# Encoder kernel: the evacuations of one plain pair moved behind the next pair's copies, and the last tile finished in three column pieces

## The chip, the cores and the metric

The kernel runs on one core of one Trainium2 chip. The metric is device time in microseconds for one launch; the number given for a kernel is the median of several runs.

## The reference

One encoder layer over two request groups, 1024 sample rows and 256 prompt rows of width 1024, all in float32. What matters here are the last two of its steps:

```python
h2 = rms_norm(x, norm_mlp_g) * (1 + scale2) + shift2
x = x + gate2 * (jnp.square(jax.nn.relu(h2 @ w_mlp_up)) @ w_mlp_down)
return rms_norm(x, final_g)      # x * rsqrt(mean(x*x) + 1e-6) * final_g
```

`w_mlp_up` is 1024 x 4096 and `w_mlp_down` 4096 x 1024. Everything ahead of them (modulation, input projection, convolution branch, attention branch, output projection) is the same in both kernels.

## The kernel before, in words

Every float32 operand of a product is split into a high part (a rounded copy, ScalarE, helper `hi_lo` line 156) and a low part (the difference, VectorE or GpSimd, line 160), and each product is three matmuls: high x high, high x low, low x high. The order of the instructions on every engine is the order in which the program emits them; there is no scheduler. Each engine works its own list in that order, and so do the two lists of transfers that SyncE (`nc.sync.dma_start`) and ScalarE (`nc.scalar.dma_start`) issue.

**The up projection** (lines 1263 to 1545) handles its 32 blocks of 128 hidden columns in pairs. The 1280 rows are three chunks: 0 and 1 of 512 rows, 2 of 256. Pairs 0 and 1 are *plain*: eight k-steps of three matmuls for each of the chunks, one bank of PSUM for each output, with `po[f, c]` for block f and chunk c, and `pm1` for chunk 2 of both blocks of pair 1. Pairs 2 to 15 (`up_pair`, line 1445) use seven products of halves instead of eight (a Strassen form): their operands are the raw pieces A and B of the weight, the sums S12 and S34 of pieces (`p_sum`, split by `p_split`), and the row operands T1, T2, T3, T4 (combinations of pieces of the activations, made by `t_first` and `t_third`). T3 is written over `Mh[1]`, `Ml[1]`, so `t_third(k)` can only run when the plain products have read those.

An evacuation `up_out` is a Relu and a Square on ScalarE from PSUM into a tile `r` (lines 1317, 1318) and one transfer issued from ScalarE's own list (line 1323); `up_out_c2` does the same for chunk 2, with two transfers (line 1329). `t_third(k)` is two sums on VectorE (`b_raw`, line 1381), a difference there (line 1415), the high copy on ScalarE (line 1392) and the low part on VectorE (line 1393, deferred until `t_lo`).

The order around the change is: `p_split(2, False)`, `t_third(0)`, `up_out_c2(1, pm1)`, `p_sum(2, True)`, `t_lo()`, `up_out(2, 0, ...)`, and then pair 2. In a pair, TensorE forms X from the first half of A, and ScalarE copies X to `p1` (line 1455); TensorE does half of the chunk 2 products (24 matmuls of 256 columns) and only then adds more products into the same bank X, for which `p1` must have been read. The products Y (S12 x T2) and V (S12 x T1) follow; VectorE reads Y with `p1` into `u2` (line 1465), and TensorE then adds S34 x T3 into the same bank Y, for which `u2` must have been read. Between the products the function `after(step)` (line 1518) emits the preparation of the same and of the next pair. In pair 2 it also emits the rest of pair 1's work:

```python
            if i == 2 and step == 0:
                up_out(3, 0, po[3, 0])
                t_third(1); t_third(2); t_lo()
            elif i == 2 and step == 1:
                t_third(3); t_lo()
            if step == 0:
                p_split(i, True)          # high half ScalarE, low half VectorE for i < 3
```

(three calls are put on one line here). `after(1)` comes behind the evacuation of X and ahead of Y.

**The down projection** (`mlp_down`, line 1567) sums over groups of hidden blocks into ten accumulators `acc[t]`, one for each tile of 128 rows. In the last group, of five blocks, `finish(t, pds)` (line 1621) also adds the two PSUM banks, multiplies by the gate `gb`, adds the residual `base[t]`, and normalises: a Square with a row sum on ScalarE (line 1608, for the last tile 1633), mean and power -0.5 on GpSimd (lines 180, 181, for the last tile 1635, 1638 and 1639) and one VectorE operation `(acc * rs) * fg` (`fin_out`, line 1617), followed by the store that SyncE issues (line 1619). The normalisation of a tile is emitted one or two tiles later. For the last tile (t = 9) the bank of columns 0 to 511 is filled first (15 matmuls of 512 columns), then that of 512 to 1023, and the VectorE steps run on each half; `fin_out(8)` stands behind them, and `fin_out(9, 2)` works and stores the last tile in two halves.

Of the kernel before, what the change touches and what calls it, by code (L numbers as in the profile page):

```python
# [13 lines left out]
D = 1024  # L14
# [11 lines left out]
EPS = 1e-6  # L26
# [44 lines left out]
def encoder_kernel(tc, x_prompt, x_sample, c_prompt, c_sample, ada_w, ada_b, norm_mix_g, w_in,  # L71
# [1357 lines left out]
        up_out(2 + fi, 1, po[2 + fi, 1])  # L1429
    p_split(2, False)  # L1430
    t_third(0)
    up_out_c2(1, pm1)
    p_sum(2, True)
    t_lo()
    up_out(2, 0, po[2, 0])

    def prod(out, w, at_, xh, xl, first, last, more=False):

# [76 lines left out]
    for i in range(2, NP):  # L1515
        last = i == NP - 1

        def after(step, i=i, last=last):
            if i == 2 and step == 0:
                up_out(3, 0, po[3, 0])  # L1520
                t_third(1)
                t_third(2)
                t_lo()
            elif i == 2 and step == 1:
                t_third(3)
                t_lo()
            if step == 0:
                p_split(i, True)
                if last:
                    wd_load(0)  # L1530
                    wd_load(1)
                    g_load(0)
                else:
                    p_load(i + 1)
            elif step == 1:
                wd_split(0) if last else p_ab(i + 1, 0)
            elif step == 2:
                g_load(1) if last else p_sum(i + 1, False)
            elif step == 3:
                g_split(0) if last else p_sum(i + 1, True)  # L1540
            elif step == 4:
                wd_split(1) if last else p_ab(i + 1, 1)
            elif not last:
                p_split(i + 1, False)
        up_pair(i, after)
# [20 lines left out]
    def mlp_down(fs, evac, between, early=0):  # L1566

        nf = len(fs)
        ws = {}
        steps = [(t, range(3)) for t in range(early)] + [(t, range(3, nf)) for t in range(early)]  # L1570
        steps += [(t, range(nf)) for t in range(early, NT)]
        banks = {}
        for n, (t, part) in enumerate(steps):
            o = t * 128
            if t not in banks:
                banks[t] = [bank("b", "dn_ps", 8) for _ in range(2)]
            pds = banks[t]
            order = [(i, hf) for i in part for hf in range(2)] if early and t == 0 else \
                [(i, hf) for hf in range(2) for i in part]
            for i, hf in order:  # L1580
                if i not in ws:
                    ws[i] = dn.pop(("W", fs[i]))
                gh, gl_ = (g[:, o:o + 128] for g in dn["G", fs[i]])
                wdh, wdl = (w[:, hf * 512:hf * 512 + 512] for w in ws[i])
                for s, (l_, r_) in enumerate(((gh, wdh), (gh, wdl), (gl_, wdh))):
                    nc.tensor.matmul(pds[hf], lhsT=l_, rhs=r_, start=(i == 0 and s == 0), stop=(i == nf - 1 and s == 2),  # L1586
                                     skip_group_check=bool(early))
            if part[-1] == nf - 1:
                evac(t, pds)
            between(n)  # L1590
        for f in fs:
            dn.pop(("G", f))
# [28 lines left out]
    def finish(t, pds):  # L1621
        gb = g2[0 if t < 8 else 1]
        if t >= 1:
            fin_norm(t - 1)
        if t == NT - 1:
            ss = co.tile([128, 4], F32, tag="sums", name="ss2", bufs=3)
            sq = fp.tile([128, D], F32, tag="sq", name="sq", bufs=2)
            for hf in range(2):
                cs = slice(hf * 512, hf * 512 + 512)
                nc.vector.tensor_add(acc[t][:, cs], acc[t][:, cs], pds[hf])  # L1630
                nc.vector.tensor_mul(acc[t][:, cs], acc[t][:, cs], gb[:, cs])
                nc.vector.tensor_add(acc[t][:, cs], acc[t][:, cs], base[t][:, cs])
                nc.scalar.activation(sq[:, cs], acc[t][:, cs], AF.Square, accum_out=ss[:, hf:hf + 1])
                if hf == 0:
                    nc.gpsimd.tensor_scalar(ss[:, 2:3], ss[:, 0:1], 1.0 / D, EPS, op0=ALU.mult, op1=ALU.add)
            fin_out(t - 1)
            rs = co.tile([128, 1], F32, tag="rs", name="rs", bufs=8)
            nc.gpsimd.tensor_scalar(rs, ss[:, 1:2], 1.0 / D, ss[:, 2:3], op0=ALU.mult, op1=ALU.add)
            nc.gpsimd.tensor_tensor(rs, rs, neghalf[:, 0:1], op=ALU.pow)
            fin[t] = rs  # L1640
            fin_out(t, 2)
            return
        for hf in range(2):
            cs = slice(hf * 512, hf * 512 + 512)
            nc.vector.tensor_add(acc[t][:, cs], acc[t][:, cs], pds[hf])
            if t >= 2 and hf == 0:
                fin_out(t - 2)
        nc.vector.tensor_mul(acc[t], acc[t], gb)
        (nc.vector if t == NT - 2 else nc.gpsimd).tensor_tensor(acc[t], acc[t], base[t], op=ALU.add)
        if t == NT - 2:  # L1650
            fin_out(t - 1)
        base_load(t + 3)

    chunks = [[0]] + [[f, f + 1] for f in range(1, NF - 5, 2)] + [list(range(NF - 5, NF))]
# [79 lines left out]
```

## Time and profile before

| what | value |
|---|---|
| median of three runs | 1894.7 us (1893.22 to 1895.27) |
| time of the profiled execution | 1894.61 us |
| its span, first to last instruction | 1892.8 us |
| TensorE matmul busy | 1842.3 us, 97% of the span |
| TensorE weight load busy | 1537.4 us, 81% |
| VectorE, ScalarE, GpSimd busy | 1082.7, 682.0, 625.6 us |
| mean granted TensorE clock | 0.991 |
| moved by DMA | 207.55 MB, 110 GB/s on average |

Engines are PE (TensorE matmul), PEld (its weight load), DVE (VectorE), ACT (ScalarE), POOL (GpSimd) and SP (SyncE); a name with q behind it is the engine's sequencer, which issues transfers. Matmuls are pipelined, so a matmul's own time is longer than the distance from its start to the next one's. In a row of the timeline the first number is the start in us from the span's start, the second the time; in brackets stands how long the engine was idle before, and what ended that. A group's idle time says who came last by the profile.

### The profile page before, as it was taken

How to read it: one execution, taken by the hardware profiler on the slowest of the kernel's cores; microseconds unless marked ns; L12 is line 12 of the kernel's file. 1: busy time of each engine (PE TensorE's matmuls, PEld its weight loads, DVE VectorE, ACT ScalarE, POOL GpSimd, SP SyncE). 2: the span in 40 equal slices, each digit the busy share in tenths (PEclk: the TensorE clock that was granted, in tenths of full speed). 3: DMA queues.
4: the chain of work that ended last, by engine and by line, in shares of the span. 5: the costliest groups of instructions: out<-in, count | busy, mean ns of one | idle time of the engine just before them, and what ended most of it. 6: DMA issues, size and time to landing. Idle time of an engine off the chain costs nothing.

```text
span 1892.8 us, 24497 instructions
## 1 busy us (share of the span) xinstructions
PE 1842.3 (97%) x9468; PEld 1537.4 (81%) x9468; DVE 1082.7 (57%) x1420; ACT 682.0 (36%) x1132; POOL 625.6 (33%) x467
## 2 busy tenths in 40 slices
PE   5999999999999999999999999999999999999998
PEld 2888777888997888877788878888888888888886
DVE  3799996524436777777555753333334555555557
ACT  3411111221346877774233454444444111111112
POOL 3321121421321343334022024333345444234443
PEclk7999999999999999999999999999999999999999
DMA  8313452227131211117632233222226332233224
GB/s 313 112 44 106 173 185 99 70 96 254 51 86 74 54 44 39 47 49 226 208 123 79 84 103 98 98 92 95 95 87 210 115 100 80 71 101 101 75 93 154
DMA packets 120934, 207.55 MB, mean 110 GB/s; under 512 B 10946, under 2 KB 78355, under 8 KB 119794
## 3 DMA queue, kind: packets, MB, share of 16 engines
q1 hardware_dynamic: 103106, 167.32, 27.6%
q10 hardware_dynamic: 17712, 38.67, 5.2%
q8 instruction: 74, 1.21, 0.3%
q14 instruction: 42, 0.34, 0.1%
HBM read 151.83 MB, written 54.12 MB: 109 GB/s over the span
## 4 chain that ended last, share of the span: by engine, by line
PE 54%; DVE 4%; DMA 3%; ACT 2%; issue 1%; POOL 1%; SPq 0%; ACTq 0%; DVEq 0%; POOLq 0%
PE dn_ps L1586 23%; PE up_ps L1442 13%; PE wo_ps L1198 4%; PE tp L866 2%; PE up_ps L330 2%; PE up_ps L329 2%; PE up_ps L328 2%; PE ops L881 1%; PE ops L880 1%; PE S L851 1%; PE S L850 1%; PE S L852 1%; DMA ga<-sig_a 1%; DMA m<-m_d 1%; DMA orr<-o_d 1%
## 5 line engine op out<-in xcount | busy, mean ns | idle before, releaser
L160 POOL TENSOR_TENSOR wl<-wr,wh 128x1024 fp32r<-128x1024 f32 (+1 forms) x100 | 232.0, 2321 | 759.6 <-ACT wh L156 729.5
L1601 DVE TENSOR_TENSOR acc<-acc,dn_ps 128x512 f32<-128x512 f32 x260 | 178.8, 688 | 174.8 <-PE dn_ps L1586 174.8
L1586 PE MATMUL dn_ps<-wh,gl 128*128 128x512 f32 x640 | 249.1, 389 | 0.9 <-POOL gl L160 0.9
L1586 PE MATMUL dn_ps<-wl,gh 128*128 128x512 f32 x640 | 249.0, 389 | 0.0
L1586 PE MATMUL dn_ps<-wh,gh 128*128 128x512 f32 x640 | 249.0, 389 | 0.0
L156 ACT ACTIVATE wh<-wr 128x1024 fp32r<-128x1024 f32 (+1 forms) x104 | 102.9, 991 | 381.8 <-PE dn_ps L1586 290.5
L412 DVE SCALAR_TENSOR_TENSOR z<-u,dwt,z 128x1310 f32<-128x1310 f32 x120 | 220.8, 1840 | 4.3
L328 PE MATMUL fma<-Hh,wh 128*128 128x512 f32 x384 | 154.7, 403 | 0.3 <-DVE Hh L158 0.3
L329 PE MATMUL fma<-Hl,wh 128*128 128x512 f32 x384 | 150.4, 392 | 2.0 <-DVE Hl L160 2.0
L330 PE MATMUL fma<-Hh,wl 128*128 128x512 f32 x384 | 150.4, 392 | 0.0
L1586 PEld LDWEIGHTS dn_ps<-wh,gl 128*128 128x128 f32 x640 | 120.1, 188 | 26.2 <-POOL gl L160 1.4
L1586 PEld LDWEIGHTS dn_ps<-wl,gh 128*128 128x128 f32 x640 | 120.1, 188 | 25.1
L1586 PEld LDWEIGHTS dn_ps<-wh,gh 128*128 128x128 f32 x640 | 120.1, 188 | 24.8
L160 DVE TENSOR_TENSOR Pl<-tp,Ph 128x512 fp32r<-128x512 f32 x144 | 92.8, 650 | 20.2 <-ACT Ph L156 19.0
L160 POOL TENSOR_TENSOR gl<-gr,gh 128x1280 fp32r<-128x1280 f32 x32 | 94.3, 2947 | 12.5 <-DMA up_d<-r 9.7
L328 PE MATMUL up_ps<-Mh,wh 128*128 128x256 f32 (+1 forms) x320 | 97.4, 304 | 0.8 <-ACT hf L266 0.8
L329 PE MATMUL up_ps<-Ml,wh 128*128 128x256 f32 (+1 forms) x320 | 97.4, 304 | 0.0
L330 PE MATMUL up_ps<-Mh,wl 128*128 128x256 f32 (+1 forms) x320 | 97.4, 304 | 0.0
L156 ACT ACTIVATE Ph<-tp 128x512 fp32r<-128x512 f32 x144 | 82.4, 574 | 35.9 <-PE tp L866 33.2
L1442 PE MATMUL up_ps<-Mh,wh 128*128 128x512 f32 x224 | 87.5, 391 | 4.3 <-ACT p L1455 2.4
L328 PEld LDWEIGHTS fma<-Hh,wh 128*128 128x128 f32 x384 | 72.5, 189 | 23.2 <-issue 5.0
L1442 PE MATMUL up_ps<-Ml,wh 128*128 128x512 f32 x224 | 87.3, 390 | 0.0
(327 smaller groups left out, 4285.4 us busy)
## 6 DMA issues: line engine op xcount, KB each, us to landing
gr<-up_d SPq DMA_DIRECT2D x32, 640.0 KB
adr<-in_ada_w_dram SPq DMA_DIRECT2D x32, 512.0 KB
wr<-in_w_mlp_up_dram SPq DMA_DIRECT2D x32, 512.0 KB
up_d<-r ACTq DMA_DIRECT2D x64, 256.0 KB
wr<-in_w_mlp_down_dram SPq DMA_DIRECT2D x32, 512.0 KB
wr<-in_w_in_dram SPq DMA_DIRECT2D x24, 512.0 KB
ar<-in_ada_w_dram SPq DMA_DIRECT2D x8, 1024.0 KB
sig_a<-sgg ACTq DMA_DIRECT2D x8, 640.0 KB
```

Source lines behind the costliest of these rows:

```text
L156: nc.scalar.activation(h, raw, AF.Copy)
L160: e.tensor_tensor(l, raw, h.bitcast(F32), op=ALU.subtract)
L328: nc.tensor.matmul(o, lhsT=wh, rhs=xh, start=first, stop=False)
L329: nc.tensor.matmul(o, lhsT=wh, rhs=xl, start=False, stop=False)
L330: nc.tensor.matmul(o, lhsT=wl, rhs=xh, start=False, stop=last)
L412: nc.vector.scalar_tensor_tensor(out=z[j], in0=u[j][:, t:t + ZW], scalar=dwt[:, j, t:t + 1], in1=z[j], op0=ALU.mult, op1=ALU.add)
L850: nc.tensor.matmul(S[:, b:b + e], lhsT=Qh[:, qs], rhs=Kh[:, kk], start=True, stop=False)
L866: nc.tensor.transpose(tp[:, i * 128:(i + 1) * 128], st_[n]["P"][i][:, k * 128:(k + 1) * 128], ident)
L1198: nc.tensor.matmul(pp[hf], lhsT=a, rhs=wo[k][b][:, hf * 512:hf * 512 + 512], start=(k == 0 and s == 0), stop=(k == KD - 1 and s == 2))
L1442: nc.tensor.matmul(out, lhsT=l_, rhs=r_[:, k, :], start=(a and s == 0), stop=(b and s == 2), skip_group_check=more)
L1586: nc.tensor.matmul(pds[hf], lhsT=l_, rhs=r_, start=(i == 0 and s == 0), stop=(i == nf - 1 and s == 2), skip_group_check=bool(early))
L1601: nc.vector.tensor_add(acc[t][:, cs], acc[t][:, cs], pds[hf])
```

## The change

In pair 2 three evacuations of pair 1 move to later places in the lists: that of chunk 2 (`up_out_c2(1, pm1)`) and of block 2 (`up_out(2, 0)`) from ahead of the pair into `after(0)` and `after(1)`, behind the T3 copies there, and that of block 3 (`up_out(3, 0)`) from the head of `after(0)` to `after(2)`. In the last tile, the second bank's products are issued as two column quarters, each over all five blocks (256 columns a matmul), and the VectorE and ScalarE steps run on a half and two quarters. Tile 8's product with `fg` moves to VectorE at the end of its own `finish`, and ScalarE scales it and SyncE stores it at the head of the last tile's `finish`. The last tile's `(acc * rs) * fg` becomes a product with `fg` on VectorE, and then a scaling of columns 512 to 1023 on ScalarE (stored from its own list) beside one of columns 0 to 511 on VectorE (stored by SyncE).

```diff
--- before.py
+++ after.py
@@ -1429,10 +1429,8 @@
         up_out(2 + fi, 1, po[2 + fi, 1])
     p_split(2, False)
     t_third(0)
-    up_out_c2(1, pm1)
     p_sum(2, True)
     t_lo()
-    up_out(2, 0, po[2, 0])
 
     def prod(out, w, at_, xh, xl, first, last, more=False):
 
@@ -1517,13 +1515,16 @@
 
         def after(step, i=i, last=last):
             if i == 2 and step == 0:
-                up_out(3, 0, po[3, 0])
                 t_third(1)
                 t_third(2)
                 t_lo()
+                up_out_c2(1, pm1)
             elif i == 2 and step == 1:
                 t_third(3)
                 t_lo()
+                up_out(2, 0, po[2, 0])
+            elif i == 2 and step == 2:
+                up_out(3, 0, po[3, 0])
             if step == 0:
                 p_split(i, True)
                 if last:
@@ -1577,6 +1578,8 @@
             pds = banks[t]
             order = [(i, hf) for i in part for hf in range(2)] if early and t == 0 else \
                 [(i, hf) for hf in range(2) for i in part]
+            if early and t == NT - 1:
+                order = [(i, 0) for i in part]
             for i, hf in order:
                 if i not in ws:
                     ws[i] = dn.pop(("W", fs[i]))
@@ -1585,6 +1588,14 @@
                 for s, (l_, r_) in enumerate(((gh, wdh), (gh, wdl), (gl_, wdh))):
                     nc.tensor.matmul(pds[hf], lhsT=l_, rhs=r_, start=(i == 0 and s == 0), stop=(i == nf - 1 and s == 2),
                                      skip_group_check=bool(early))
+            if early and t == NT - 1:
+                for lo in (512, 768):
+                    for i in part:
+                        gh, gl_ = (g[:, o:o + 128] for g in dn["G", fs[i]])
+                        wdh, wdl = (w[:, lo:lo + 256] for w in ws[i])
+                        for s, (l_, r_) in enumerate(((gh, wdh), (gh, wdl), (gl_, wdh))):
+                            nc.tensor.matmul(pds[1][:, lo - 512:lo - 256], lhsT=l_, rhs=r_, start=(i == 0 and s == 0),
+                                             stop=(i == nf - 1 and s == 2), skip_group_check=True)
             if part[-1] == nf - 1:
                 evac(t, pds)
             between(n)
@@ -1625,20 +1636,29 @@
         if t == NT - 1:
             ss = co.tile([128, 4], F32, tag="sums", name="ss2", bufs=3)
             sq = fp.tile([128, D], F32, tag="sq", name="sq", bufs=2)
-            for hf in range(2):
-                cs = slice(hf * 512, hf * 512 + 512)
-                nc.vector.tensor_add(acc[t][:, cs], acc[t][:, cs], pds[hf])
+            eps = co.tile([128, 1], F32, name="eps")
+            nc.scalar.activation(base[t - 1], base[t - 1], AF.Copy, scale=fin[t - 1])
+            nc.sync.dma_start(y_rows(t - 1), base[t - 1])
+            for i, cs in enumerate((slice(0, 512), slice(512, 768), slice(768, 1024))):
+                p0 = cs.start % 512
+                nc.vector.tensor_add(acc[t][:, cs], acc[t][:, cs], pds[cs.start // 512][:, p0:p0 + cs.stop - cs.start])
                 nc.vector.tensor_mul(acc[t][:, cs], acc[t][:, cs], gb[:, cs])
                 nc.vector.tensor_add(acc[t][:, cs], acc[t][:, cs], base[t][:, cs])
-                nc.scalar.activation(sq[:, cs], acc[t][:, cs], AF.Square, accum_out=ss[:, hf:hf + 1])
-                if hf == 0:
-                    nc.gpsimd.tensor_scalar(ss[:, 2:3], ss[:, 0:1], 1.0 / D, EPS, op0=ALU.mult, op1=ALU.add)
-            fin_out(t - 1)
+                nc.scalar.activation(sq[:, cs], acc[t][:, cs], AF.Square, accum_out=ss[:, i:i + 1])
+                if i == 0:
+                    nc.gpsimd.tensor_scalar(eps, ss[:, 0:1], 1.0 / D, EPS, op0=ALU.mult, op1=ALU.add)
+                elif i == 1:
+                    nc.gpsimd.tensor_scalar(eps, ss[:, 1:2], 1.0 / D, eps, op0=ALU.mult, op1=ALU.add)
             rs = co.tile([128, 1], F32, tag="rs", name="rs", bufs=8)
-            nc.gpsimd.tensor_scalar(rs, ss[:, 1:2], 1.0 / D, ss[:, 2:3], op0=ALU.mult, op1=ALU.add)
+            nc.gpsimd.tensor_scalar(rs, ss[:, 2:3], 1.0 / D, eps, op0=ALU.mult, op1=ALU.add)
             nc.gpsimd.tensor_tensor(rs, rs, neghalf[:, 0:1], op=ALU.pow)
             fin[t] = rs
-            fin_out(t, 2)
+            fg_x = base[t]
+            nc.vector.tensor_mul(fg_x, acc[t], fg)
+            nc.scalar.activation(fg_x[:, 512:1024], fg_x[:, 512:1024], AF.Copy, scale=rs)
+            nc.scalar.dma_start(y_rows(t)[:, 512:1024], fg_x[:, 512:1024])
+            nc.vector.tensor_scalar(fg_x[:, 0:512], fg_x[:, 0:512], rs, None, op0=ALU.mult)
+            nc.sync.dma_start(y_rows(t)[:, 0:512], fg_x[:, 0:512])
             return
         for hf in range(2):
             cs = slice(hf * 512, hf * 512 + 512)
@@ -1649,6 +1669,7 @@
         (nc.vector if t == NT - 2 else nc.gpsimd).tensor_tensor(acc[t], acc[t], base[t], op=ALU.add)
         if t == NT - 2:
             fin_out(t - 1)
+            nc.vector.tensor_mul(base[t], acc[t], fg)
         base_load(t + 3)
 
     chunks = [[0]] + [[f, f + 1] for f in range(1, NF - 5, 2)] + [list(range(NF - 5, NF))]
```

## Rows read from the trace of the kernel before

**Rows 1.** The waits of TensorE over the whole span: who waited for whom, total us, times, longest us.

```profile
PE up_ps L1442 <- ACT p L1455: 2.4, 1, 2.4
...
PE up_ps L1442 <- DVE u L1465: 1.9, 1, 1.9
```

**Rows 2.** The timeline of TensorE's matmuls at the start of pair 2.

```profile
1097.73 0.28 PE L328 MATMUL up_ps<-Mh,wh 128*128 128x256 f32 x1
...
1100.48 0.28 PE L330 MATMUL up_ps<-Mh,wl 128*128 128x256 f32 x1
1103.12 0.50 PE L1442 MATMUL up_ps<-Mh,wh 128*128 128x512 f32 x1 [2.36 <-ACT p L1455]
...
1111.19 0.39 PE L1442 MATMUL up_ps<-T1h,wl 128*128 128x512 f32 x1
1113.52 0.47 PE L1442 MATMUL up_ps<-Mh,wh 128*128 128x512 f32 x1 [1.95 <-DVE u L1465]
```

**Rows 3.** The timeline of ScalarE in the same stretch (ACTq is its list of transfers).

```profile
1098.62 0.58 ACT L1317 ACTIVATE r<-up_ps 128x512 f32<-128x512 f32 x1
...
1099.89 0.81 ACTq L1329 DMA_DIRECT2D up_d<-r  x2
1100.80 0.60 ACT L1317 ACTIVATE r<-up_ps 128x512 f32<-128x512 f32 x1 [0.94 <-ACT r L1318]
...
1102.47 0.60 ACT L1455 ACTIVATE p<-up_ps 128x512 f32<-128x512 f32 x1 [0.40 <-ACT r L1318]
...
1106.62 0.63 ACT L1392 ACTIVATE Mh<-br 128x512 fp32r<-128x512 f32 x1 [1.36 <-DVE br L1415]
1107.15 1.04 ACT L156 ACTIVATE wh<-sr 128x1024 fp32r<-128x1024 f32 x1
```

**Rows 4.** The timeline of VectorE in the same stretch.

```profile
1101.09 0.69 DVE L1415 TENSOR_TENSOR br<-br,u 128x512 f32<-128x512 f32 x1
...
1105.29 0.69 DVE L1393 TENSOR_TENSOR Ml<-br,Mh 128x512 fp32r<-128x512 f32 x1 [2.18 <-ACT Mh L1392]
1105.89 0.69 DVE L1415 TENSOR_TENSOR br<-br,u 128x512 f32<-128x512 f32 x1
...
1108.23 1.23 DVE L160 TENSOR_TENSOR wl<-sr,wh 128x1024 fp32r<-128x1024 f32 x1 [0.25 <-ACT wh L156]
...
1112.69 0.68 DVE L1465 TENSOR_TENSOR u<-up_ps,p 128x512 f32<-128x512 f32 x1
```

**Rows 5.** The timeline of VectorE over the last two tiles.

```profile
1879.43 1.23 DVE L1649 TENSOR_TENSOR acc<-acc,fx 128x1024 f32<-128x1024 f32 x1
1880.57 1.28 DVE L1617 SCALAR_TENSOR_TENSOR fx<-acc,rs,fg 128x1024 f32<-128x1024 f32 x1
1881.77 0.68 DVE L1630 TENSOR_TENSOR acc<-acc,dn_ps 128x512 f32<-128x512 f32 x1
...
1883.21 0.69 DVE L1632 TENSOR_TENSOR acc<-acc,fx 128x512 f32<-128x512 f32 x1
1884.25 0.69 DVE L1630 TENSOR_TENSOR acc<-acc,dn_ps 128x512 f32<-128x512 f32 x1 [0.35 <-PE dn_ps L1586]
...
1885.69 0.69 DVE L1632 TENSOR_TENSOR acc<-acc,fx 128x512 f32<-128x512 f32 x1
...
1888.38 1.41 DVE L1617 SCALAR_TENSOR_TENSOR fx<-acc,rs,fg 128x512 f32<-128x512 f32 x2 [0.80 <-POOL rs L1639]
```

**Rows 6.** The timeline of TensorE's last matmul.

```profile
1883.82 0.39 PE L1586 MATMUL dn_ps<-wh,gl 128*128 128x512 f32 x1
```

**Rows 7.** The timeline of ScalarE at the last tile.

```profile
1886.42 0.63 ACT L1633 ACTIVATE sq<-acc 128x512 f32<-128x512 f32 x1 [1.71 <-DVE acc L1632]
1886.96 0.19 ACT L1633 ACTIVATION_READ_ACCUMULATOR sq<-acc 128x1 f32 x1
```

**Rows 8.** The timeline of GpSimd over the last two tiles.

```profile
1882.26 0.55 POOL L181 TENSOR_TENSOR rs<-rs,neghalf 128x1 f32<-128x1 f32 x1
...
1887.32 0.40 POOL L1638 TENSOR_SCALAR rs<-ss 128x1 f32<-128x1 f32 x1 [2.33 <-ACT sq L1633]
1887.80 0.55 POOL L1639 TENSOR_TENSOR rs<-rs,neghalf 128x1 f32<-128x1 f32 x1
```

**Rows 9.** Groups of instructions of VectorE with the shapes kept apart: line, engine, operation, tiles, shapes, count; then busy us, mean ns of one, and idle time before them.

```profile
L1226 DVE TENSOR_SCALAR x<-x,rs 128x1024 f32<-128x1024 f32 x10 | 7.5, 751 | 12.8 <-DMA x_d<-x 12.1 <-POOL rs L181 0.7
...
L1150 DVE TENSOR_TENSOR ga<-ao_ps,ga 128x256 f32<-128x256 f32 x8 | 3.4, 422 | 5.8 <-DMA ga<-sig_a 5.8
```

**Rows 10.** The same for ScalarE.

```profile
L266 ACT ACTIVATE hf<-xt_ps,mod,A 128x512 f32<-128x512 f32 x16 | 12.4, 775 | 11.0 <-POOL Hl L160 4.2 <-PE xt_ps L323 2.9 <-PE fma L330 2.1
...
L156 ACT ACTIVATE Qh<-qc 128x256 fp32r<-128x256 f32 x8 | 3.3, 416 | 0.0
```

**Rows 11.** The timeline of SyncE's list of transfers at the end (one row for three stores: of tile 8, and of the two halves of tile 9).

```profile
1887.61 2.54 SPq L1619 DMA_DIRECT2D out_dram<-fx  x3
```

**Rows 12.** Stretches at the end: length in us, busy us of PE, PEld, DVE, ACT and POOL (with the number of instructions), then TensorE's granted clock as a share of full speed, the busy share of the DMA engines, and GB/s.

```profile
1887.40:1888.00 0.60, 0.00 (x0) 0.00 (x0) 0.18 (x1) 0.00 (x0) 0.52 (x2) 0.71 0.00 0
1889.90:1891.40 1.50, 0.00 (x0) 0.00 (x0) 0.00 (x0) 0.00 (x0) 0.00 (x0) 0.50 0.90 350
```

**Rows 13.** The same for two stretches near the start.

```profile
40.00:45.00 5.00, 4.81 (x16) 4.11 (x17) 4.41 (x8) 3.17 (x5) 4.54 (x8) 0.55 0.59 166
45.00:50.00 5.00, 5.00 (x30) 4.18 (x29) 4.78 (x6) 2.69 (x5) 3.43 (x4) 1.00 0.13 31
```

## The prediction

> **What bounds the kernel now.** TensorE does: it is busy for 97% of the span. So I first read its waits, to see where it stops, then the timelines of the two places that the change touches. The list of waits holds, for the products of the pairs, only two rows, one stop each [rows 1]. Both lie at the start of pair 2. TensorE's timeline shows them: the last 256-column matmul starts at 1100.48, 24 of them have come at (1100.48 - 1097.73) / 23 = 0.12 us each, so the next should start at 1100.60 and starts at 1103.12; and again nothing starts between 1111.19 and 1113.52 [rows 2]. ScalarE's timeline says why the first: X is finished by about 1098, but `p1` runs at 1102.47, behind the evacuations of chunk 2 and of block 2 [rows 3]. VectorE's says why the second: `u2` runs at 1112.69, behind the whole chain of T3 copies [rows 4]. The other place is the end. There TensorE's last matmul starts at 1883.82 and ends at 1884.21 [rows 6]; behind it come three VectorE steps on 512 columns, the Square, two small GpSimd steps, two VectorE products, two stores [rows 5, 7, 8, 11]. Everything that the change can touch is thus the 2.4 and 1.9 us of two stops and the 8.6 us from the last matmul to the span's end at 1892.8.
>
> **Part 1, the three evacuations.** The path that sets the end of the second stop is followed instruction by instruction, with the distances of the trace.
>
> *First stop.* ScalarE now comes to `p1` where it came to chunk 2's evacuation, at 1098.62, and has read X by 1099.2; TensorE wants X again at 1100.60. The stop goes: 1103.12 - 1100.60 = 2.5 us.
>
> *Second stop.* TensorE would then finish V 2.5 us sooner, with its last matmul starting at 1108.7 instead of 1111.19, and want Y. It still waits for `u2`, which VectorE does in its order behind all T3 copies. That chain in the new order: the difference of `t_third(1)` starts at 1101.09 as before, since VectorE was busy without a break up to there. ScalarE is free now, so its high copy starts at 1101.8. In the old run VectorE stood idle 2.18 us ahead of the low part at 1105.29, so it can do it at 1105.29 - 2.18, less the 0.09 by which successive steps overlap: 1103.02. The difference of `t_third(2)` follows after 0.60 (1103.62), its high copy on ScalarE 0.73 later (1104.35) [rows 3, 4]. So far 2.3 us are won. But the next on ScalarE's list is now `up_out_c2(1, pm1)`, because `after(0)` emits it ahead of `p_split(2, True)`. It can start 0.53 after the copy (as 1107.15 does after 1106.62), at 1104.88, and with its two transfers it holds ScalarE for 1100.80 - 1098.62 = 2.18. The high half of S34 starts at 1107.06; it started at 1107.15 [rows 3]. From there nothing differs up to `u2`: low half at 1108.23, `t_third(3)`, its copies, `u2` at 1112.69, TensorE at 1113.52 [rows 2, 4], each 0.09 earlier. The evacuation of X, between them on ScalarE in both orders, is done before the last copy is asked for.
>
> So 2.5 us of stop go and 2.4 come back at the next: **-0.1 us**. Bounds: -2.3 if something lets the split of S34 go ahead of chunk 2's evacuation, 0 if the two transfers take a little more.
>
> *What else moves.* `up_out(2, 0)` and its transfer now stand ahead of pair 3's first weight copy on ScalarE, and `up_out(3, 0)` behind it: 1102.47 - 1100.80 = 1.67 us each [rows 3]. GpSimd waits for that copy, and TensorE wants the result only when it starts pair 3, after 36 matmuls at about 0.23 and 24 at 0.12, some 11 us behind 1113.4: cost nothing; without that cover 1.7. The banks of the three outputs and the tiles `r` are held 6 to 13 us longer; their next users are in pair 3, or behind at least five later tiles: nothing. The four moved transfers write blocks that the down projection reads much later: nothing.
>
> **Part 2, the last tile.**
>
> *TensorE:* 15 matmuls of 512 columns become 30 of 256, 30 x 0.12 = 3.6 against 15 x 0.23 = 3.4: the last ends at about 1884.4. That is not on the path, as follows.
>
> *VectorE ahead of the last tile:* the product of tile 8 with `fg` (1024 columns) is new, at 1881.77, where the first addition of tile 9 stood. The like at 1879.43 holds VectorE for 1880.57 - 1879.43 = 1.14, so the last tile's first addition starts at 1882.91 and the addition of the residual at 1883.21 + 1.14 = 1884.35 [rows 5]. VectorE's only idle time here was 0.35, ahead of the second half's 1884.25. Then the two quarters. Before, the step behind an independent 512-column one came after 0.61, so the first quarter's addition starts at 1884.96, when TensorE has ended. A 256-column step takes 0.42 [rows 9], a dependent one follows after 0.45, an independent one after 0.33: the second quarter's addition starts at 1884.96 + 2 x 0.45 + 0.33 = 1886.19, its last step at 1887.09, and that ends at 1887.51. Before it was 1885.69 + 0.69 = 1886.38 [rows 5]: 1.13 later. The quarters were to let VectorE start sooner; it is now too late for them to matter.
>
> *Square, GpSimd:* the Square of a quarter takes 0.42 instead of 0.63 [rows 7, 10], 0.21 less; the row sum and GpSimd's two steps stay as they are [rows 7, 8]. The earlier partial means are hidden. From the start of the Square to VectorE's first product it was 1888.38 - 1886.42 = 1.96; now 1.75, from 1887.55: the scale is there at **1889.30, 0.92 later**.
>
> *Scaling:* before, two products one after the other, 1.41, end at 1889.79 [rows 5]. Now VectorE does one 512-column scaling: the 1024-column one takes 0.75 [rows 9], so between 0.38 and 0.69; I take 0.45: 1889.75. ScalarE beside it: 512 columns without a scale operand 0.63 [rows 7], with scale and bias operands 0.78 [rows 10]; I take 0.78, the shape with an operand: 1890.1. The product with `fg` of the last tile (1.2) lies beside the Square and GpSimd.
>
> *Stores:* the first half's was issued at about 1889.15 and the last at 1889.81 (the list ends at 1890.15, an issue takes 0.34) [rows 11]; they moved at 1889.9 to 1891.4 with the DMA engines 0.90 busy at 350 GB/s [rows 12]. Now the first goes at 1889.77, 0.62 later, the second from ScalarE at 1890.1, 0.3 later. If the engines' rate binds, the end moves by up to 0.6; if only the last issue counts, by 0.3. Between these I take 0.5, since the two follow each other more closely than before. The Trainium skill, "DMA: Bandwidth & Descriptors", section "Issuing engines are not separate DMA queues", says that transfers started from several engines run on the same DMA engines and save only issue time. By that the end moves by the larger figure, +0.5; with two independent paths it would be +0.3; the busy share above agrees with the page. The store of tile 8, which started at 1887.61 [rows 11], now goes at about 1884.3: ScalarE can scale the tile once the product ends at 1883.0 and the scale is there (1882.26 + 0.55 [rows 8]); the Square that queues behind it is not ready before 1885.0. It was not in the way before, as its data were through by the time that the halves moved.
>
> Together **+0.5 us**, bounds +0.2 (VectorE's scaling at its shortest, the stores overlapping) and +0.9 (VectorE's at 0.69, the stores in line).
>
> **Sum.** -0.1 + 0.5 = +0.4. The profiled execution took 1894.61, the median of the runs is 1894.7: 1895.0 by the one, 1895.1 by the other. I say 1895.0.
>
> **The rivals.**
>
> *A. One long stop cools TensorE (slower).* Before, the stops were 2.36 and 1.95 us with a burst between. Now TensorE would stand idle from about 1109.0 to 1113.4 in one piece, 4.4. At the end of the trace the last matmul ends at 1884.21 and the granted clock is 0.71 on average over 1887.4 to 1888, a fall from 1.0 to 0.5 at about 1887.65 [rows 6, 12], 3.4 us behind the last matmul. So a fall to the lower level, 1.2 GHz, ahead of 1113.4 is possible. Near the start TensorE worked 4.8 of 5 us at a mean of 0.55 before it got 1.0 [rows 13]: some 4.5 us at half speed, 2.2 us lost, so 1897.2. It decides over more than 0.2% only if the low level lasts (3.8 - 0.4) x 2 = 6.8 us. Against it: that fall came after an idle time with nothing behind it, and here only 1 us is left beyond 3.4. The Trainium skill, "TensorE: Matmul & The Clock Gate", section "HAM oscillation — how this bites in real kernels", warns that waits between bursts of matmuls return TensorE to half clock each time; that speaks against this change, and no row of this stretch shows it yet. Chance 0.16.
>
> *B. The first stop's gain is kept (faster).* If the split of S34 is not held up by chunk 2's evacuation, the second stop ends 2.3 earlier: 1895.0 - 2.2 = 1892.8. For it: up to `t_third(2)` the chain does run 2.3 ahead. Against it: ScalarE works its list in order, and that order is in the code. Chance 0.08.
>
> *C. The end is not set by VectorE (a little faster).* If the new product of tile 8 found a gap, the end would go 1.1 sooner: 1893.9. VectorE has no such gap in the rows. Chance 0.08.
>
> **How the numbers follow.** The forecast has 0.68. All cases but the far end of A lie within 0.2%, 3.8 us, which is about what a measurement of this kernel can tell from no change; the runs of before spread over 2 us themselves. Faster by more would need B, C and more: 0.03. Slower by more: A with a long low level, 0.05. Same: 0.92. The range goes from B's side, 1893.0, to A's price, 1897.2.
>
> **What would show it.** In the new trace: `p1` at about 1098.6 and no stop at 1100.6; one stop of TensorE of about 4.4 us ahead of S34 x T3, ended by `u2`, with the high half of S34 on ScalarE at 1107.1; granted clock 1.0 around it. At the end: VectorE without idle time from 1880 to 1887.5, the power step on GpSimd ending near 1889.3, the two stores at 1889.8 and 1890.1. I am wrong if the second stop ends before 1112 or the last Square starts before 1887.

## The result, and the profile after

The changed kernel takes **1921.53 us** (1920.95 to 1922.27) against 1894.06 beside it (1893.22 to 1895.27): ratio **1.0147 [1.0132, 1.0161]**, 27.5 us slower. The forecast was 1895.0, with an upper end of 1897.2. One execution of run 7 below took 2302.66 us at a mean granted clock of 0.75 and is left out of that run's median. The head of the changed kernel's page: span, and the busy time of each engine.

```profile
span 1920.5 us, 24536 instructions
...
PE 1868.7 (97%) x9483; PEld 1539.7 (80%) x9483; DVE 1080.0 (56%) x1423; ACT 685.4 (36%) x1136; POOL 626.5 (33%) x468
```

TensorE is busy 26.4 us longer (1842.3 before), with 15 matmuls more by the diff. At some 0.12 us each these cannot be it. Nor can its waits: for the products of the pairs the list of waits has one row now, where it had two [rows 1].

```profile
PE up_ps L1440 <- DVE u L1463: 3.2, 1, 3.2
```

So I set stretches side by side that the change does not touch. Each row is a stretch, its length, and the busy time and number of instructions of PE, PEld, DVE, ACT, POOL, then granted clock, DMA share and GB/s. Ahead of it all lies the convolution branch (110 to 190), in the middle the pairs, at the back the down projection (1500 to 1800). Before:

```profile
110.00:190.00 80.00, 80.00 (x419) 65.99 (x418) 78.61 (x47) 9.33 (x11) 15.70 (x6) 1.00 0.28 85
1180.00:1380.00 200.00, 200.00 (x1064) 173.21 (x1063) 61.49 (x72) 86.19 (x120) 77.68 (x34) 1.00 0.30 97
1500.00:1800.00 300.00, 300.00 (x1326) 248.39 (x1325) 151.39 (x222) 47.64 (x44) 117.39 (x45) 1.00 0.27 88
```

After, with three stretches around the end of the stop in pair 2:

```profile
110.00:190.00 80.00, 80.00 (x413) 64.69 (x412) 78.61 (x48) 9.30 (x11) 18.59 (x6) 1.00 0.25 75
1180.00:1380.00 200.00, 200.00 (x1047) 169.90 (x1046) 60.67 (x72) 85.28 (x118) 76.52 (x32) 1.00 0.29 94
1500.00:1800.00 300.00, 300.00 (x1288) 240.94 (x1287) 146.99 (x215) 47.69 (x44) 116.82 (x44) 1.00 0.28 87
1118.00:1120.00 2.00, 0.00 (x0) 0.00 (x0) 1.30 (x3) 1.73 (x3) 0.00 (x0) 1.00 0.00 0
1120.00:1122.00 2.00, 1.66 (x4) 1.41 (x5) 1.49 (x3) 1.57 (x4) 0.45 (x1) 0.50 0.33 131
1122.00:1124.00 2.00, 2.00 (x7) 1.56 (x7) 0.00 (x0) 0.62 (x1) 1.93 (x1) 0.65 0.25 96
```

TensorE never stops in the first three, the clock is 1.00 in both kernels, and yet fewer matmuls fit: one every 300 / 1288 = 0.2329 us instead of 300 / 1326 = 0.2262 in the down projection (+2.9%), 1.6% fewer in the pairs, 1.4% in the convolution branch, a thousand microseconds ahead of the first moved instruction. The loss is spread over the kernel, at the full clock, without a wait.

The groups with shapes kept apart say which matmuls (count, busy us, mean ns of one). Before, and then after:

```profile
L329 PE MATMUL fma<-Hl,wh 128*128 128x512 f32 x384 | 150.4, 392 | 2.0 <-DVE Hl L160 2.0
L1198 PE MATMUL wo_ps<-woh,Ml 128*128 128x512 f32 x160 | 49.6, 391 | 0.0
L329 PE MATMUL fma<-Zl,wh 128*128 128x512 f32 x64 | 25.0, 391 | 0.0
L1586 PE MATMUL dn_ps<-wh,gl 128*128 128x512 f32 x640 | 249.1, 389 | 0.9 <-POOL gl L160 0.9
```

```profile
L329 PE MATMUL fma<-Hl,wh 128*128 128x512 f32 x384 | 152.4, 397 | 0.0
L1198 PE MATMUL wo_ps<-woh,Ml 128*128 128x512 f32 x160 | 49.5, 391 | 0.0
L329 PE MATMUL fma<-Zl,wh 128*128 128x512 f32 x64 | 25.0, 391 | 0.0
L1589 PE MATMUL dn_ps<-wh,gl 128*128 128x512 f32 x635 | 250.9, 395 | 0.8 <-POOL gl L160 0.8
```

The first and the last became 5 or 6 ns longer, the two between stayed. (Products of 256 columns with the operands of the first row did not become longer: a mean of 283 ns before and 281 after.) In the built program's addresses the pools stand in two stacks, one from the left end of SBUF and one from the right. `wh`, `wl`, `Zh`, `Zl` lie on the left; `Hh`, `Hl`, `Mh`, `Ml`, `gh`, `gl`, `woh` on the right. The products that became longer are those with one operand on each side. And all that the left side holds behind the pool `co` begins 32 bytes later than before (`wh` at 28960 instead of 28928), because of one line of the diff: `eps = co.tile([128, 1], F32, name="eps")`. Its 4 bytes take 32 in each partition.

*Theory P (place):* the 32 bytes between the two sides cost the time. *Rival Q:* the moved and split work costs it, by a path that these stretches do not show.

The places that I had predicted, in the timeline after (start, time; in brackets the idle time and what ended it):

```profile
1105.91 0.60 ACT L1453 ACTIVATE p<-up_ps 128x512 f32<-128x512 f32 x1 [0.26 <-PE up_ps L1440]
...
1111.29 0.63 ACT L1392 ACTIVATE Mh<-br 128x512 fp32r<-128x512 f32 x1 [1.90 <-DVE br L1415]
1111.83 0.58 ACT L1317 ACTIVATE r<-up_ps 128x512 f32<-128x512 f32 x1
...
1113.96 1.06 ACT L156 ACTIVATE wh<-sr 128x1024 fp32r<-128x1024 f32 x1 [0.89 <-ACT r L1318]
...
1119.51 0.68 DVE L1463 TENSOR_TENSOR u<-up_ps,p 128x512 f32<-128x512 f32 x1
...
1120.34 0.77 PE L1440 MATMUL up_ps<-Mh,wh 128*128 128x512 f32 x1 [3.22 <-DVE u L1463]
...
1908.30 1.22 DVE L1672 TENSOR_TENSOR fx<-acc,fg 128x1024 f32<-128x1024 f32 x1
1908.52 1.05 POOL L180 TENSOR_SCALAR rs<-ss 128x1 f32<-128x1 f32 x1 [5.00 <-ACT sq L1619]
...
1914.11 0.42 ACT L1647 ACTIVATE sq<-acc 128x256 f32<-128x256 f32 x1 [0.74 <-DVE acc L1646]
1914.11 1.23 DVE L1657 TENSOR_TENSOR fx<-acc,fg 128x1024 f32<-128x1024 f32 x1
1914.79 0.68 POOL L1653 TENSOR_SCALAR rs<-ss,eps 128x1 f32<-128x1 f32 x1 [0.99 <-ACT sq L1647]
...
1916.13 0.49 DVE L1660 TENSOR_SCALAR fx<-fx,rs 128x512 f32<-128x512 f32 x1 [0.80 <-POOL rs L1654]
```

`p1` no longer stands behind two evacuations [rows 3]: ScalarE is idle for 0.26 us ahead of it and waits for X itself. The high copy of S34 (1113.96) starts 2.67 us after the T3 copy (1111.29), since chunk 2's evacuation stands between them. One stop is left, ended by `u2`, and the clock is 0.50 behind it.

### The profile page after: what moved, and what is told of

The parts are those of the page before. It is cut to its first block, busy times and chain, and to the rows that moved or that the text cites. A ratio compares the mean times of both kernels' runs of the same rounds, so it can differ in the third digit from the quotient of the medians.

```text
span 1920.5 us, 24536 instructions
## 1 busy us (share of the span) xinstructions
PE 1868.7 (97%) x9483; PEld 1539.7 (80%) x9483; DVE 1080.0 (56%) x1423; ACT 685.4 (36%) x1136; POOL 626.5 (33%) x468
## 3 DMA queue, kind: packets, MB, share of 16 engines
q1 hardware_dynamic: 102962, 167.05, 27.5%
## 4 chain that ended last, share of the span: by engine, by line
PE 54%; DVE 5%; DMA 3%; ACT 2%; issue 1%; POOL 1%; ACTq 0%; SPq 0%; POOLq 0%; DVEq 0%
PE dn_ps L1589 23%; PE up_ps L1440 13%; PE wo_ps L1198 4%; PE tp L866 2%; PE up_ps L328 1%; PE up_ps L330 1%; PE up_ps L329 1%; PE ops L881 1%; PE ops L880 1%; PE S L850 1%; PE S L851 1%; PE S L852 1%; DMA m<-m_d 1%; DMA ga<-sig_a 1%; ACT P L858 1%
## 5 line engine op out<-in xcount | busy, mean ns | idle before, releaser
L1440 PE MATMUL up_ps<-Mh,wl 128*128 128x512 f32 x224 | 89.1, 398 | 0.0
```

The source lines that it names most:

```text
L1440: nc.tensor.matmul(out, lhsT=l_, rhs=r_[:, k, :], start=(a and s == 0), stop=(b and s == 2), skip_group_check=more)
```

## The experiments

Each ratio is to the kernel before, run on the same chip, with its 95% interval.

**1. The change without the new tile** (from after):

```diff
-            eps = co.tile([128, 1], F32, name="eps")
+            eps = ss[:, 3:4]
```

> The changed kernel with the whole change, but the running mean of the last tile kept in the unused fourth column of the tile of row sums instead of in the new tile `eps`. The new tile takes 32 bytes a partition in the first pool of the left side and moves every later tile of that side by 32 bytes (the weight parts from offset 28928 to 28960) against those of the right side, which stay. Theory P (place): the 27.5 us come from that move; without it 1894 to 1897 us, distance of two 512-column matmuls in the down projection back at 0.227 us (0.233 to 0.235 in the changed kernel). Rival C (the changed instructions themselves: 30 matmuls instead of 15, the order, the long stop): 1921 us as before.

Measured 1897.74 against 1895.1: 1.0015 [1.0006, 1.0025]. Of the 27.5 us 2.6 are left, as theory P has it, though 0.7 us more than its range.

**2. Before, with the tile alone**, which nothing uses:

```diff
+            co.tile([128, 1], F32, name="eps")
```

> The kernel before with one line more: an unused tile of one float32 column in the same pool; no instruction is added or moved. Theory P: 1920 to 1922 us, with 512-column matmuls of the convolution, up and down projections 1.5 to 3% further apart. Rival C: 1894 us.

Measured 1919.79: 1.0129 [1.0114, 1.0144], **+24.7 us** without one instruction of the change. With run 1 this makes 24.7 + 2.6 = 27.3 of 27.5. Rival Q falls for all but the 2.6. The down projection, 1500 to 1800:

```profile
1500.00:1800.00 300.00, 300.00 (x1287) 240.98 (x1287) 147.38 (x215) 47.66 (x44) 116.83 (x44) 1.00 0.27 87
```

**3. After, with the right side moved as well.** A padding tile stands in front of everything on the right side; eight floats less move that side by the same 32 bytes.

```diff
-    al.tile([128, 56], F32, name="al_pad")
+    al.tile([128, 48], F32, name="al_pad")
```

> The changed kernel, new tile and all, but the unused tile at the start of the right side 32 bytes smaller, so that the right side moves by 32 bytes too. Every tile then starts 32 bytes past a multiple of 64, left and right alike. Theory P in its form R (the two operands of a matmul must have the same place modulo 64): 1894 to 1897 us. Form A (each tile must start at a multiple of 64): at least 1921 us. Rival C: 1921 us.

Measured 1899.01: 1.0022 [1.0013, 1.0032]; the tile is still there, and the distance is back:

```profile
1500.00:1800.00 300.00, 300.00 (x1325) 248.51 (x1324) 151.78 (x221) 47.70 (x44) 117.40 (x45) 1.00 0.28 88
```

So it is the place of the two operands to each other, and not either's own place. The time is 1.3 us above run 1's and 2 us past the range; why, no run shows.

**4. After, with a tile of 64 bytes:**

```diff
-            eps = co.tile([128, 1], F32, name="eps")
+            eps = co.tile([128, 16], F32, name="eps")[:, 0:1]
```

> The changed kernel with the new tile 64 bytes wide instead of 4 (it takes 64 in the place of 32): the left side moves by 64 bytes against the right. Theory P with a period of 64 bytes: 1894 to 1897 us. With a period of 128 or more: between 1900 and 1930. Rival C: 1921 us.

Measured 1907.31: 1.0073 [1.0055, 1.0091], between the two. 64 bytes are not a period.

**5. Part 1 alone** (before, with the three moves of the evacuations as in the diff):

> The kernel before with the three moved evacuations alone; the last tile as before, no new tile. Theory G (the stop is given back and TensorE's clock falls): one stop of about 4.5 us ahead of S34 x T3, granted clock 0.50 for 3 to 4 us from its end, so -0.1 for the stops and about +2 for the clock: 1896.5 to 1897.5 against 1895.1. Rival N (the moved evacuations are neutral and the clock costs nothing): within 0.5 us of before. Rival W (they win the first stop): 1892.5 to 1893.

Measured 1896.78 against 1895.0: 1.0012 [1.0003, 1.0020], +1.8. TensorE's stop, from the timeline:

```profile
1114.12 0.47 PE L1440 MATMUL up_ps<-Mh,wh 128*128 128x512 f32 x1 [4.48 <-DVE u L1463]
```

and the clock behind it:

```profile
1108.00:1114.00 6.00, 1.63 (x8) 1.02 (x6) 4.44 (x7) 3.66 (x6) 0.00 (x0) 1.00 0.19 71
1114.00:1118.00 4.00, 3.88 (x10) 3.12 (x11) 1.26 (x2) 2.17 (x3) 2.37 (x1) 0.57 0.34 131
1118.00:1120.00 2.00, 2.00 (x16) 1.88 (x16) 1.24 (x2) 0.00 (x0) 0.00 (x0) 1.00 0.00 0
```

The stop is the 4.4 predicted, and 4 us at 0.57 lose 4 x 0.43 = 1.7.

**6. The same, with twelve matmuls in the stop** whose result nothing uses, between V and `after(2)`:

```diff
+        if i == 2:
+            prod(up_bank(), w["S12"], s0, *TT_[1], True, True, True)
```

> The same with 12 extra matmuls of 512 columns in pair 2 between V and S34 x T3, into a bank that nobody reads (S12 x T1 once more): 2.7 us of work for TensorE inside the stop of 4.5. Theory G: the clock stays at 1.00, and with more work the kernel gets faster than f1 by 1.5 to 2.5 us, about 1895. If the clock costs nothing: equal to f1 or slower by up to 0.3 us.

Measured 1893.97: 0.9997 [0.9988, 1.0006], 2.8 us *faster* than run 5 with more work. The wait for `u2` is 1.75 now, and the clock stays up:

```profile
1112.00:1118.00 6.00, 5.60 (x36) 5.12 (x37) 4.07 (x7) 3.33 (x6) 2.40 (x1) 1.00 0.24 90
```

Part 1's loss is thus the clock, not the order of the work. The fall accounts for 1.7 of the 2.8; the other 1.1 no row explains.

**7. Part 2 alone** (before, with the last-tile edits of the diff, `eps` in the spare column):

> The kernel before with the second part alone (quarters, tile 8 scaled early, the last scaling on two engines; the running mean in a spare column, no new tile). By the steps of the prediction VectorE sets the end and gets the last scale 0.9 us later, the stores end 0.5 later: +0.5 us, between +0.2 and +0.9, so 1895.6. Rival: the quarters win and the end comes 0.5 to 1 us sooner: 1894.3.

Measured 1895.73: 1.0007 [0.9998, 1.0016], +0.7, which the times cannot tell from nothing. The trace can: from the product of tile 7 to the end of the span the tail is 1894.6 - 1881.22 = 13.4 us long, and it was 1892.8 - 1880.57 = 12.2 in the trace of before [rows 5]. Runs 1, 3, 4 and after have 13.4 too, runs 5, 6 and 8, with the old tail, 12.2.

```profile
1881.22 1.28 DVE L1627 SCALAR_TENSOR_TENSOR fx<-acc,rs,fg 128x1024 f32<-128x1024 f32 x1
```

Pair 2 is as before in this run, and yet its clock fell, behind the first stop. The fall cost nothing: TensorE then waited 0.49 for `u2` instead of 1.95, and from the end of the first stop to that of the second it is 1114.12 - 1103.72 = 10.40 us here and 1113.52 - 1103.12 = 10.40 in the trace of before [rows 2], which has no fall. In runs 13 and 14 the same fall is found, and the same 10.40.

```profile
1103.72 0.80 PE L1442 MATMUL up_ps<-Mh,wh 128*128 128x512 f32 x1 [2.39 <-ACT p L1455]
1114.12 0.47 PE L1442 MATMUL up_ps<-Mh,wh 128*128 128x512 f32 x1 [0.49 <-DVE u L1465]
```

```profile
1104.00:1106.00 2.00, 2.00 (x5) 1.54 (x6) 0.11 (x1) 1.42 (x3) 0.00 (x0) 0.50 0.91 334
```

**8. Part 1 with the split of S34 first** (before, edited):

```diff
-    up_out_c2(1, pm1)
...
-    up_out(2, 0, po[2, 0])
...
+            if step == 0:
+                p_split(i, True)
             if i == 2 and step == 0:
-                up_out(3, 0, po[3, 0])
-                t_third(1)
-                t_third(2)
+                for k in range(1, 4):
+                    t_third(k)
                 t_lo()
             elif i == 2 and step == 1:
-                t_third(3)
-                t_lo()
+                up_out_c2(1, pm1)
+                up_out(2, 0, po[2, 0])
+            elif i == 2 and step == 2:
+                up_out(3, 0, po[3, 0])
             if step == 0:
-                p_split(i, True)
```

> The kernel before with the evacuations moved further: after(0) does the split of S34 first and then all three T3 copies, after(1) evacuates chunk 2 and block 2, after(2) block 3. Theory G: the first stop goes (2.5 us), ScalarE's work no longer delays the T3 copies, u2 runs at about 1109.2, so the second stop shrinks from 1.95 us to between 0.5 and 1.2, and the clock stays at 1.00: 3 to 4 us less than before, 1891 to 1892. Rival (the copies on VectorE bound the stop wherever the evacuations stand): 1894 to 1895.

Measured **1892.43**: 0.9990 [0.9981, 0.9999], 2.6 us less than before and, by a narrow margin, the only version that beats both kernels. It fell short of its forecast, of a stop of 0.5 to 1.2 and a clock that stays up: its profile, taken of its slowest run (1894.93), shows a stop of 1.80 and a fall of the clock behind it. That is not so in every execution: run 9, whose pair 2 is the same, has a stop of 1.82 and no fall.

```profile
1112.22 0.47 PE L1440 MATMUL up_ps<-Mh,wh 128*128 128x512 f32 x1 [1.80 <-DVE u L1463]
```

```profile
1114.00:1117.00 3.00, 3.00 (x10) 2.43 (x10) 0.42 (x1) 2.12 (x3) 0.00 (x0) 0.50 0.40 145
```

**9. Run 8 with a mended tail:** the three pieces of the diff, but tile 8's `fin_out` behind them as before, and only columns 512 to 1023 multiplied by `fg` ahead of the scale.

```diff
-            fin_out(t, 2)
...
+            nc.vector.tensor_mul(fg_x[:, 512:1024], acc[t][:, 512:1024], fg[:, 512:1024])
+            nc.scalar.activation(fg_x[:, 512:1024], fg_x[:, 512:1024], AF.Copy, scale=rs)
...
+            nc.vector.scalar_tensor_tensor(out=fg_x[:, 0:512], in0=acc[t][:, 0:512], scalar=rs, in1=fg[:, 0:512],
+                                           op0=ALU.mult, op1=ALU.mult)
```

> Both parts mended, no new tile: the order of f4 for the evacuations, and the last tile in three pieces with its scaling on two engines, but tile 8's product and store left behind the last tile's steps on VectorE, as before, and only columns 512 to 1023 multiplied by fg ahead of the scale. By the steps: VectorE ends the last tile's chain where it did before, the Square is 0.2 us shorter, the two scalings lie side by side (0.7 instead of 1.41): the end 0.5 us sooner than before. With f4's 2.6 us: about 3 us less than before, 1891.5 to 1892.5. If the early product of tile 8 was not what held the last tile up: no better than f4, 1892.5 to 1893.5.

Measured 1893.93 against 1894.11: 1.0000 [0.9991, 1.0009], a miss. The stop in pair 2, and GpSimd's mean step beside VectorE's two products, in the timeline:

```profile
1110.59 0.47 PE L1440 MATMUL up_ps<-Mh,wh 128*128 128x512 f32 x1 [1.82 <-DVE u L1463]
...
1878.10 1.28 DVE L1627 SCALAR_TENSOR_TENSOR fx<-acc,rs,fg 128x1024 f32<-128x1024 f32 x1
...
1884.47 1.27 DVE L1627 SCALAR_TENSOR_TENSOR fx<-acc,rs,fg 128x1024 f32<-128x1024 f32 x1
1884.59 0.42 ACT L1644 ACTIVATE sq<-acc 128x256 f32<-128x256 f32 x1 [0.74 <-DVE acc L1643]
...
1885.27 1.13 POOL L1651 TENSOR_SCALAR rs<-ss 128x1 f32<-128x1 f32 x1 [0.99 <-ACT sq L1644]
...
1885.67 0.68 DVE L1655 TENSOR_TENSOR fx<-acc,fg 128x512 f32<-128x512 f32 x1
```

The mean step took 1.13 us, and 0.40 before [rows 8], so the scale came 2.48 behind the start of the last Square instead of 1.96: the work put beside the step made the step longer. The Square itself started 1884.59 - 1878.10 = 6.49 behind the product of tile 7 and not 1886.42 - 1880.57 = 5.85 [rows 5, 7], so the two quarters also cost VectorE time. From that product to the span's end at 1891.6 it is 13.5 us, 1.3 more than before; this takes back half of what run 8 won.

**10 to 15. The place alone.** Before, with an unused tile of another size as in run 2, or with the right side moved as in run 3.

> The kernel before with an unused tile of 128 bytes: the left side moves by 128 bytes against the right. Theory P with a period of 128 bytes: within 0.2% of before. With a longer period: 1900 us or more.

> The kernel before with an unused tile of 64 bytes, nothing else (e4 had the whole change as well and took 1907). Theory P: what e4 took over e1 (1907.3 - 1897.7 = 9.6 us) comes from the place alone, so 1904 to 1906. If e4's time came from the place and the change together: near 1895.

> The kernel before with the unused tile at the start of the right side 32 bytes smaller: the right side moves up by 32 bytes, the left stays at multiples of 64. Theory P in its form R (the difference between the two operands counts): 1915 to 1925 us, like e2, in which the left side was moved. Form L (only the place of the left side, with the weight parts, counts): 1895 us.

> The kernel before with an unused tile of 256 bytes. In the kernel before all operands of the three long products, left and right, start at 256 past a multiple of 512. Theory P with a period of 256 bytes: 1894 to 1896 us. With a period of 512: slow, 1900 to 1925.

> The kernel before with an unused tile of 512 bytes. Theory P with a period of 512 bytes (or 256): 1894 to 1896 us. If there is no such period and any move away from the placement before costs: 1905 or more.

> The kernel before with an unused tile of 480 bytes: modulo 512 the left side then stands 32 bytes behind the right, as in the run that moved the right side up by 32. Period of 512: 1915 to 1919 us, as there (1916.6). Without a period: not told.

| edit of before | us | ratio to before |
|---|---|---|
| left + 32 (run 2) | 1919.79 | 1.0129 [1.0114, 1.0144] |
| left + 64 | 1905.36 | 1.0064 [1.0050, 1.0078] |
| left + 128 | 1917.85 | 1.0125 [1.0111, 1.0138] |
| left + 256 | 1895.05 | 1.0001 [0.9991, 1.0010] |
| left + 480 | 1917.89 | 1.0123 [1.0108, 1.0139] |
| left + 512 | 1894.87 | 1.0002 [0.9993, 1.0011] |
| right moved by 32 | 1916.63 | 1.0120 [1.0106, 1.0134] |

Where the two sides agree again modulo 256 bytes the loss is gone, though more is moved; 480 behaves as 32 does, moving the right side alone as the left alone. The convolution branch with 64 bytes, and the down projection with 64 and with 256:

```profile
110.00:190.00 80.00, 80.00 (x413) 64.71 (x412) 78.61 (x47) 9.31 (x11) 17.89 (x6) 1.00 0.26 78
1500.00:1800.00 300.00, 300.00 (x1312) 246.19 (x1311) 149.90 (x218) 47.66 (x44) 117.61 (x44) 1.00 0.27 87
```

```profile
1500.00:1800.00 300.00, 300.00 (x1325) 248.51 (x1324) 151.99 (x221) 47.69 (x44) 116.72 (x45) 1.00 0.27 87
```

Theory P stands in this form: a 512-column matmul follows the last one sooner when its two operands start at the same place modulo 256 bytes, as far as the offsets tried can tell. The 64 bytes cost less than half above all because of the down projection: the convolution branch loses as much as with 32 (413 matmuls for 419), the pairs nearly as much (1050 in 200 us, for 1064 before and 1047 after), and the down projection about a third (1312, for 1326 and 1288). In the first two the stationary operand of a matmul lies on the left, in the down projection on the right; whether that is why was not tested. What in the chip makes the place count, no run here shows.

## Why the prediction was wrong

**The step that failed** is the sentence that bounds the change: "Everything that the change can touch is thus the 2.4 and 1.9 us of two stops and the 8.6 us from the last matmul to the span's end". The change also moved the operands of thousands of matmuls. In part 2 I costed what the partial means do ("The earlier partial means are hidden") and not the tile that holds them. The size can be worked out from the spacing. The down projection has 3 x 640 matmuls of 512 columns: 1920 x (0.2329 - 0.2262) = 12.9 us. The convolution branch has 3 x 384 with `Hh` or `Hl`, whose starts came 226 to 229 ns apart and now come 231 to 235, some 6 ns more: 6.9 us. That leaves 24.7 - 12.9 - 6.9 = 4.9 for the pairs and the rest. All rivals were priced from the same two places, so none could hold the result.

**What is left without the tile,** +2.6 (run 1), was forecast as +0.4 and lies just past the end of the range (1897.2 is 2.5 above the median). Step by step:

- *First stop:* right. TensorE no longer waits for `p1`.
- *Second stop:* right. It takes back what the first gave, since the split of S34 stands behind chunk 2's evacuation: 4.48 in run 5, 4.4 forecast.
- *Rival A, the clock:* this happened, and I gave it 0.16. Its price was sound: 2.2 forecast, and run 5 lost 1.8. Its chance was not: I argued that the one fall in the trace had nothing behind it and that the stop barely reaches as far. Every profile with one stop here of 3.2 us or more shows the fall (five of five: after, runs 1, 3, 4, 5), and run 6 shows that without it the loss is gone. The section of the Trainium skill that I cited ("TensorE: Matmul & The Clock Gate", "HAM oscillation — how this bites in real kernels") spoke against the change, and the trace of run 5 agrees with it (0.57 for 4 us behind the stop). The trace of before, which I went by, has no fall at all, and not every execution of its order is like that: the clock fell behind a first stop of 2.39 in runs 7, 13 and 14, where the second stop took the loss up. In the change the only stop is the last, and nothing behind it does.
- *Rival B* asked what happens if the split of S34 is not held up. In this change it is; made so in run 8, it gives 2.6, near the 2.2 that I had put on it.
- *The last tile:* +0.7 by the times of run 7 and +1.2 by its trace, for +0.5 with an upper end of +0.9. The mechanism was as forecast; two terms were too small. The rows of run 7, whose tail began 0.65 later than in the trace of before (the product of tile 7 at 1881.22, 1880.57 in [rows 5]):

```profile
1888.22 0.42 ACT L1646 ACTIVATE sq<-acc 128x256 f32<-128x256 f32 x1 [0.74 <-DVE acc L1645]
...
1888.91 0.68 POOL L1652 TENSOR_SCALAR rs<-ss 128x1 f32<-128x1 f32 x1 [0.99 <-ACT sq L1646]
...
1890.25 0.48 DVE L1659 TENSOR_SCALAR fx<-fx,rs 128x512 f32<-128x512 f32 x1 [0.80 <-POOL rs L1653]
```

The last Square was forecast for 1887.55 + 0.65 = 1888.20 and came at 1888.22. The scale was forecast for 1889.95 and came at 1890.25, since GpSimd's mean took 0.68 beside the new VectorE product (1888.22 to 1889.45 here) where I had left it at 0.40 [rows 8]: the term "GpSimd's two steps stay as they are" was too small by 0.3. The stores' data moved in one block (DMA busy share 0.98 to 1.06 from 1891.6 to 1892.8), as by the larger of my two figures, 0.6, and not the 0.5 that I took; with the 0.3 this makes 0.9. The remaining 0.2 or 0.3 of the 1.2 came behind the data, and no row explains it.

## What to carry to other kernels

A new tile, however small, moves all that is allocated behind it: compare the addresses of the two built programs before costing the instructions, keep the two operands of a 512-column matmul at the same place modulo 256 bytes, and put a scratch value into a spare column. Taking away the first of two stops only helps if the next link of the chain does not queue behind the work that was moved; here the split had to go first (run 8), and two short stops joined into a long one also cost the clock, with no later stop to take the loss up. When a kernel slows down, look at a stretch that the change does not touch before looking at the one that it does.

## What the runs showed of the hardware

- The distance between 512-column matmuls whose operands lie in different stacks rose by up to 3% (0.2262 to 0.2329 us in the down projection) when the operands' places differed by 32 or 128 bytes modulo 256, and did not with 256 or 512. The Trainium skill, "TensorE: Matmul & The Clock Gate", section "Step-by-step: what each phase is for", gives the stationary and the moving operand a read port each, independent of one another; by that the relative place should not matter. The measurement decides, and the reason stays open.
- GpSimd's step on one column took 0.19 us beside a VectorE sum with one operand in SBUF and one in PSUM (at 1881.99, beside 1881.77 in [rows 5]), and 0.40 [rows 8], 0.68, 1.05 and 1.13 beside VectorE products with both operands in SBUF. In these four it ended 0.05 to 0.14 us behind the end of VectorE's product, so the 0.40 of before held a wait too. The Trainium skill, "GPSIMD Engine Reference", section "8. Key points", names contention of the two engines where a VectorE instruction has two SBUF inputs; the trace agrees. Two rows of before:

```profile
1881.99 0.19 POOL L180 TENSOR_SCALAR rs<-ss 128x1 f32<-128x1 f32 x1 [4.82 <-ACT sq L1608]
```

```profile
1886.30 1.28 DVE L1617 SCALAR_TENSOR_TENSOR fx<-acc,rs,fg 128x1024 f32<-128x1024 f32 x1
```

- TensorE's clock fell to 0.50 behind a stop of 1.80 us (run 8's profile) and behind stops of 2.39 (runs 7, 13, 14), and not behind 1.82 in run 9, whose pair 2 is run 8's, or behind 2.36 and 1.95 in the profile of before, whose pair 2 is that of runs 7, 13 and 14. So for stops of this length the same order of work came out either way; what decides it, these runs leave open.
